# Index-key gathers of the decode tokens: begun in the last output blocks of the first feed-forward part

## The chip, the cores and the metric

The kernel runs on one core of a Trainium2 chip. The metric is the device time of one execution in microseconds (us). A core has five engines with a queue of instructions each: PE (matmuls, with its weight loads shown as PEld), DVE (elementwise on vectors), ACT (activations, also issues DMAs), POOL (elementwise, and the gathers by index) and SP (issues the weight DMAs here). Engines wait for each other by semaphores alone.

## What is computed

One layer for 256 prompt tokens and 8 decode tokens that share all weights: a half-step feed-forward part, a projection into retention, sparse attention, an indexer and gates, then the mixing and a second half-step feed-forward part.

```python
def layer_forward(x, pos, ret_state0, ret_chunk, sparse_attn, p):
    x = x + 0.5 * swiglu(rms_norm(x, ffn1_norm), ffn1_w1, ffn1_w2)
    h = rms_norm(x, mix_norm)
    rq, rk, rv, rg, aq, ak, av, iq, ik, iw, g_ret, g_att = split_cols(h @ w_in)
    ret_out, ret_state = retention(rq, rk, rv, rg, ret_state0, pos, ret_chunk, ret_norm, w_ret_out)
    ...
    att = sparse_attn(aq, ak, av, iq, iw, ik)
    merged = jax.nn.sigmoid(g_ret) * ret_out + jax.nn.sigmoid(g_att) * (att @ w_att_out)
    x = x + merged @ w_o
    x = x + 0.5 * swiglu(rms_norm(x, ffn2_norm), ffn2_w1, ffn2_w2)
```

For a decode token the sparse attention scores all 2048 earlier positions with the indexer, whose keys lie in pages of 128 positions, and the page table says which:

```python
    past_ki = pool_ki[layer, page_table].reshape(db, past, IDX_DIM)
    ki_all = jnp.concatenate([past_ki, ki], axis=1)
    idx, valid = indexer_select(qi, wi, ki_all, q_pos, n_keep)
```

## The kernel before, in words

All activations lie transposed: 128 features on the partitions, 264 tokens in the free dimension, 2048 features in 16 such blocks. `quad` (line 147) gives a tile of four blocks out of a pool of 23 equal buffers that X, the normed inputs (`hi`, `lo`), the hidden values (`hh`, `hl`), the index keys (`kt`), and the projected IQ, RK and so on share.

`mblock` (line 237) makes one output block. For every eight rows of 128 weights SP loads a piece (`wr`, L247), ACT rounds it to the high part (`wh`, L248), DVE subtracts for the low part (`wl`, L249), and PE runs three matmuls per 128 rows (L252 to L254: high by high, low by high, high by low) into one of three result buffers in PSUM (`psm`, line 137). Loads and splits carry a priority that lets them run ahead, with four buffers each.

`ffn` (line 306) goes through 44 hidden blocks in three chunks (16, 16, 12). A chunk makes its hidden blocks, two projections of 16 rows each, and then 16 output blocks m with the chunk's rows (12 in the last chunk, thus 36 matmuls a block). The function handed in, `out1` (line 346), adds the result to X[m] (L348, DVE), and in the last chunk also makes block m of the next normed input (`mixn.add`: ACT L283, DVE L284) and of its sum of squares (`mixn.square`: ACT L291, then POOL adds it into `acc`, L292).

Behind the feed-forward part comes the projection, one `mixblock` of 48 matmuls per output block: first the ik block, then `mixn.done()`, which turns `acc` into `rstd` by a matmul, two activations (L258, L259) and three operations on DVE (L262 to L264); POOL multiplies `rstd` into `cosr` and `sinr` (L383, L384). Every later block is multiplied by `rstd` as it is taken from PSUM. Eight iq blocks follow (L395 into IQ), eight rk blocks with a rotary step that ends in an addition on POOL (L876 into RK), eight rq blocks, and so on.

The index keys of the 8 decode tokens, 16 pages each, come by 64 gathers on POOL (L365, `load_kt`): a gather fetches one page for two tokens, 128 rows of 512 bytes, into one of eight `kt` tiles of eight gathers each. Their order is `kt_order`. In the source five gathers stand behind each iq block (40) and eight behind each of the first three rk blocks (24). Their addresses (`kix`) are there from the start of the kernel. The first readers are the scoring matmuls of `decode_index` (L499), which is stepped from the fourth rk block on.

The order in which each engine takes its instructions is settled before the run by the framework's planner, from the source's order, the priorities and its own estimates of durations. An instruction whose inputs are there may be moved ahead of others; a tile's first writer also needs a free buffer.

Of the kernel before, what the change touches and what calls it, by code (L numbers as in the profile page):

```python
# [19 lines left out]
P = 128  # L20
# [16 lines left out]
PG = 128  # L37
# [85 lines left out]
def layer(ctx: ExitStack, tc: tile.TileContext, xT, gains, consts, dmat, didx, pt, state, cidx, ck, cv,  # L123
          w1a, w2a, wik, win, wro, wao, wo, w1b, w2b,
          yT, o_st, o_k, o_v, o_ik, o_sts):
    nc = tc.nc
# [16 lines left out]
    def nm(s):  # L143
        cnt[0] += 1
        return f"{s}_{cnt[0]}"

    def quad(dt=F32, shape=(P, 4, T), s="q"):
        return qpool.tile(list(shape), dt, tag="q", name=nm(s))
# [4 lines left out]
    def wt(s="w", shape=(P, T), dt=F32, tag="w", bufs=8):  # L153
        return work.tile(list(shape), dt, tag=tag, name=nm(s), bufs=bufs)

    def mt(s, shape=(P, 384), dt=F32):
        return work.tile(list(shape), dt, tag="m", name=nm(s), bufs=8)

    def st(shape, dt=F32, tag="s", bufs=4):
        return small.tile(list(shape), dt, tag=tag, name=nm(tag), bufs=bufs)  # L160
# [57 lines left out]
    kix = cpool.tile([P, 4, NPG], I32, name="kix")  # L218
# [12 lines left out]
    def ahead():  # L231
        return tc.high_priority(offset=AHEAD)
# [73 lines left out]
    def ffn(norm, w1, w2, out, early=0, tick=None):  # L306
        for ci, (j0, j1) in enumerate(CHUNKS):
            n = j1 - j0
            hh, hl = Blocks(n, F32R, "hh"), Blocks(n, F32R, "hl")
            for j in range(j0, j1):  # L310
                pg = mblock(w1[2 * j], KB, norm.hi, norm.lo)
                if j < early:
                    c = wt("c")
                    nc.scalar.activation(c, pg, AF.Copy)
                    pg = c
                if j == 0:
                    rstd = norm.done()
                g = wt("g")
                nc.vector.tensor_mul(g, pg, rstd)
                s = wt("s")  # L320
                nc.scalar.activation(s, g, AF.Silu)  # L321
                s2 = wt("s2")
                nc.gpsimd.tensor_mul(s2, s, rstd)  # L323
                pu = mblock(w1[2 * j + 1], KB, norm.hi, norm.lo)
                if j < early - 1:
                    c = wt("c")
                    nc.scalar.activation(c, pu, AF.Copy)
                    pu = c
                h = wt("h")
                nc.vector.tensor_mul(h, pu, s2)  # L330
                split(h, hh[j - j0], hl[j - j0])
                if tick:
                    tick()
            for m in range(KB):
                ps = mblock(w2[m][:, j0:j1, :], n, hh, hl)
                out(m, ps, ci == len(CHUNKS) - 1)
# [6 lines left out]

    mixn = Norm("gm")

    def out1(m, ps, last):
        with ahead():
            nc.vector.scalar_tensor_tensor(X[m], ps, 0.5, X[m], op0=ALU.mult, op1=ALU.add)  # L348
        if last:
            with ahead():  # L350
                mixn.add(m, X[m])
                mixn.square(m, X[m])
            if m % 4 == 3:
                nc.scalar.dma_start(xs[:, m - 3:m + 1, :], X.t[m // 4])

    ffn(norm, w1a, w2a, out1, early=1)

    KT = [[quad(shape=(P, 1024 + h), s="kt") for h in range(2)] for _ in range(4)]
    kt_order = [(p, 8 * h + i) for h in range(2) for p in range(4) for i in range(8)]

    def load_kt(n):
        for _ in range(n):
            p, pg = kt_order.pop(0)
            o = (pg % 8) * PG
            nc.gpsimd.indirect_dma_start(out=KT[p][pg // 8][:, o:o + PG], out_offset=None, in_=cidx,  # L365
                                         in_offset=bass.IndirectOffsetOnAxis(ap=kix[:, p, pg:pg + 1], axis=0))


    def mixblock(src, m=P):
        return mblock(src, KB, mixn.hi, mixn.lo, m)  # L370
# [22 lines left out]
    for i in range(8):  # L393
        ps = mixblock(blocks["iq", i])
        nc.vector.tensor_mul(IQ[i], ps, rstd)  # L395
        load_kt(5)

    queues = {}
    slack = dict(a=60, b=100, c=130)
# [17 lines left out]
    def step(**rates):  # L417
        for n, r in rates.items():
            q = queues[n]
            q[1] += r  # L420
            while q[1] >= 1.0:
                q[1] -= 1.0
                run_one(n)
# [49 lines left out]
    def decode_index():  # L473
        for p in range(4):
            for s in range(2):
                r = slice(64 * s, 64 * s + 64)
                nc.vector.tensor_copy(KT[p][1][r, 1024:1025], ik2[r, TP + 2 * p + s:TP + 2 * p + s + 1])
        qs = st([P, NB, IH], tag="qs", bufs=1)
# [14 lines left out]
        for c0, w in spans:  # L493
            pi = aux()
            half, o = (0, c0) if c0 < 1024 else (1, c0 - 1024)
            with ahead():
                for p in range(4):
                    q2 = qs[:, 2 * p:2 * p + 2, :].rearrange("p b h -> p (b h)")
                    nc.tensor.matmul(pi[32 * p:32 * p + 32, :w], q2, KT[p][half][:, o:o + w], start=True, stop=True)  # L499
            rl = mt("drl", (P, w))  # L500
# [370 lines left out]
    def rotary(ps, out, mul):  # L871
        a, b = wt("ra"), wt("rb")
        nc.vector.scalar_tensor_tensor(a, ps, mul, cosr, op0=ALU.mult, op1=ALU.mult)
        nc.vector.scalar_tensor_tensor(b[:64], ps[64:], mul, sinr[64:], op0=ALU.mult, op1=ALU.mult)
        nc.vector.scalar_tensor_tensor(b[64:], ps[:64], mul, sinr[:64], op0=ALU.mult, op1=ALU.mult)
        nc.gpsimd.tensor_add(out, a, b)  # L876
# [146 lines left out]
    for i in range(RH):  # L1023
        ps = mixblock(blocks["rk", i])
        rotary(ps, RK[i], SCALE)
        if kt_order:
            load_kt(min(8, len(kt_order)))
        step(a=1.5, b=2 if i > 2 else 0)
    lo_pool[0] = (1, 2)
    for i in range(RH):  # L1030
# [79 lines left out]
    for i in range(16):  # L1110
# [3 lines left out]
        s = wt("s")  # L1114
# [124 lines left out]
```

## Time and profile before

| | us |
|---|---|
| median of 3 runs | 2736.94 |
| lowest and highest | 2730.61, 2738.26 |
| profiled execution | 2738.78 |
| its span, first to last instruction | 2736.7 |
| PE busy in it | 2634.1 |
| POOL busy in it | 658.3 |

The span is that of the profiled execution alone. The share of busy time is a mean over the whole span; where an engine makes others late is seen in a stretch, from the count of its instructions, the waits ahead of them, and the granted clock of PE (1.00 is 2.4 GHz, 0.50 is 1.2 GHz).

### The profile page before, as it was taken

To read this page: it belongs to the slowest core of one execution; us is meant where nothing else is said; L and a number is where in the kernel's file an instruction comes from. 1 tells how busy PE (TensorE), PEld (TensorE's weight loads), DVE (VectorE), ACT (ScalarE), POOL (GpSimd) and SP (SyncE) were. 2 spreads that over 40 slices of the span, in tenths; PEclk is the share of its full clock that TensorE was granted. 3 is DMA by queue.
4 is the path that set the end of the run, shared out by engine and by line. 5 is a ranking of instruction groups with operands and counts; after the bars stand their busy time and mean duration, and the time that the engine had idled before them with its cause. 6 is when DMAs were issued, how large, how long until landed. Compare 5 with 4: busy or idle time off the path is not lost. (4 is left out here: it accounts for less than half of the span.)

```text
span 2736.7 us, 51339 instructions
## 1 busy us (share of the span) xinstructions
PE 2634.1 (96%) x21207; PEld 2594.1 (95%) x21207; DVE 1561.2 (57%) x2288; ACT 1173.8 (43%) x1557; POOL 658.3 (24%) x459
## 2 busy tenths in 40 slices
PE   7999999999997899999997999999999999999999
PEld 7999999999996699899887989999999999999999
DVE  6555555545553488644699744566655555555554
ACT  5443344334452333353535754444544334433443
POOL 3110011001135443326377243231111101110110
PEclk9999999999997899999998999999999999999999
DMA  6556555655564344456686656666576656765655
GB/s 214 182 181 182 181 183 180 184 178 184 172 222 132 106 157 160 140 174 229 216 274 217 198 190 217 203 203 220 177 235 228 216 183 226 234 215 183 214 170 171
DMA packets 173963, 529.08 MB, mean 193 GB/s; under 512 B 22704, under 2 KB 43760, under 8 KB 173728
## 3 DMA queue, kind: packets, MB, share of 16 engines
q1 hardware_dynamic: 140320, 466.28, 52.7%
q10 hardware_dynamic: 27504, 43.92, 4.9%
q0 software_dynamic: 5904, 15.59, 1.7%
q8 instruction: 166, 2.72, 0.4%
q14 instruction: 69, 0.57, 0.1%
HBM read 504.12 MB, written 21.60 MB: 192 GB/s over the span
## 5 line engine op out<-in xcount | busy, mean ns | idle before, releaser
L248 ACT ACTIVATE wh<-wr 128x1024 fp32r<-128x1024 f32 x866 | 902.4, 1043 | 1314.0 <-PE ps L253 839.1
L249 DVE TENSOR_TENSOR wl<-wr,wh 128x1024 fp32r<-128x1024 f32 (+2 forms) x798 | 993.4, 1246 | 672.2 <-ACT wh L248 651.1
L254 PE MATMUL ps<-hi,wl 128*128 128x264 f32 x4624 | 1329.3, 288 | 29.2 <-DVE wl L249 16.5
L252 PE MATMUL ps<-hi,wh 128*128 128x264 f32 x4624 | 1328.5, 287 | 29.1 <-issue 11.9
L253 PE MATMUL ps<-lo,wh 128*128 128x264 f32 x4624 | 1332.8, 288 | 11.2 <-issue 9.4
L254 PEld LDWEIGHTS ps<-hi,wl 128*128 128x128 f32 x4624 | 877.7, 190 | 39.8 <-DVE wl L249 19.8
L252 PEld LDWEIGHTS ps<-hi,wh 128*128 128x128 f32 x4624 | 879.6, 190 | 33.6 <-issue 19.2
L253 PEld LDWEIGHTS ps<-lo,wh 128*128 128x128 f32 x4624 | 878.4, 190 | 21.3 <-issue 17.1
L254 PE MATMUL ps<-hh,wl 128*128 128x264 f32 x1408 | 398.8, 283 | 0.0
L253 PE MATMUL ps<-hl,wh 128*128 128x264 f32 x1408 | 398.5, 283 | 0.0
L252 PE MATMUL ps<-hh,wh 128*128 128x264 f32 x1408 | 398.3, 283 | 0.0
L323 POOL TENSOR_TENSOR s<-s,rstd 128x264 f32<-128x264 f32 x88 | 116.9, 1329 | 1009.8 <-ACT s L321 1009.8
L253 PEld LDWEIGHTS ps<-hl,wh 128*128 128x128 f32 x1408 | 264.6, 188 | 0.0
L252 PEld LDWEIGHTS ps<-hh,wh 128*128 128x128 f32 x1408 | 264.5, 188 | 0.0
L254 PEld LDWEIGHTS ps<-hh,wl 128*128 128x128 f32 x1408 | 264.3, 188 | 0.0
L249 POOL TENSOR_TENSOR wl<-wr,wh 128x1024 fp32r<-128x1024 f32 x68 | 166.9, 2459 | 299.7 <-ACT wh L248 251.1
L805 POOL TENSOR_TENSOR pr<-qb,kb 128x1024 f32<-128x1024 f32 x32 | 86.0, 2705 | 60.0 <-DMA qb<-rows 51.6
L938 POOL TENSOR_TENSOR kv<-ku,rvs 128x512 f32<-128x512 f32 x32 | 33.6, 1051 | 219.6 <-DMA ku<-rows 206.4
L940 DVE SCALAR_TENSOR_TENSOR su<-su,kv 128x256 f32<-128x256 f32 x64 | 24.4, 422 | 98.2 <-POOL kv L938 98.2
L292 POOL TENSOR_TENSOR acc<-acc,sq 128x264 f32<-128x264 f32 x45 | 40.8, 906 | 154.0 <-ACT sq L291 153.1
L330 DVE TENSOR_TENSOR h<-ps,s 128x264 f32<-128x264 f32 x88 | 38.0, 432 | 64.5 <-PE ps L254 61.1
L253 PE MATMUL ps<-alo,wh 128*128 128x264 f32 x256 | 72.7, 284 | 0.0
(317 smaller groups left out, 2356.7 us busy)
## 6 DMA issues: line engine op xcount, KB each, us to landing
wr<-win SPq DMA_DIRECT2D x224, 512.0 KB
wr<-w1a SPq DMA_DIRECT2D x176, 512.0 KB
wr<-w1b SPq DMA_DIRECT2D x176, 512.0 KB
wr<-w2a SPq DMA_DIRECT2D x80, 512.0 KB
wr<-w2b SPq DMA_DIRECT2D x80, 512.0 KB
wr<-wro SPq DMA_DIRECT2D x32, 512.0 KB
wr<-wao SPq DMA_DIRECT2D x32, 512.0 KB
wr<-wo SPq DMA_DIRECT2D x32, 512.0 KB
```

What stands on the lines that cost most here:

```text
L248: nc.scalar.activation(wh[:, :n, :m], wr[:, :n, :m], AF.Copy)
L249: eng.tensor_sub(wl[:, :n, :m], wr[:, :n, :m], wh[:, :n, :m])
L252: nc.tensor.matmul(ps[:m, :T], wh[:, k, :m], hi[g], start=g == 0, stop=False)
L253: nc.tensor.matmul(ps[:m, :T], wh[:, k, :m], lo[g], start=False, stop=False)
L254: nc.tensor.matmul(ps[:m, :T], wl[:, k, :m], hi[g], start=False, stop=g == nk - 1)
L292: nc.gpsimd.tensor_add(self.acc, self.acc, sq)
L323: nc.gpsimd.tensor_mul(s2, s, rstd)
L330: nc.vector.tensor_mul(h, pu, s2)
L805: nc.gpsimd.tensor_mul(pr, qb, k.to_broadcast([P, 2, 4, P]))
L938: nc.gpsimd.tensor_mul(kv, k[:, :, None, :].to_broadcast([P, 2, 2, P]), v.to_broadcast([P, 2, 2, P]))
L940: nc.vector.scalar_tensor_tensor(s[:, i], s[:, i], g1[h + i], kv[:, i], op0=ALU.mult, op1=ALU.add)
```

## The change

`load_kt`, its list and its eight tiles move ahead of `out1`; a tile is now taken from the pool when its first gather is issued, not all eight at once. `out1` issues two gathers per output block of the last chunk (32 in 16 blocks), an iq block three and not five (24 in eight blocks), and an rk block up to three and not eight (8 in three blocks). Order, addresses and targets of the gathers stay.

```diff
     mixn = Norm("gm")
 
+    KT = [[None, None] for _ in range(4)]
+    kt_order = [(p, 8 * h + i) for h in range(2) for p in range(4) for i in range(8)]
+
+    def load_kt(n):
+        for _ in range(min(n, len(kt_order))):
+            p, pg = kt_order.pop(0)
+            o = (pg % 8) * PG
+            if KT[p][pg // 8] is None:
+                KT[p][pg // 8] = quad(shape=(P, 1024 + pg // 8), s="kt")
+            nc.gpsimd.indirect_dma_start(out=KT[p][pg // 8][:, o:o + PG], out_offset=None, in_=cidx,
+                                         in_offset=bass.IndirectOffsetOnAxis(ap=kix[:, p, pg:pg + 1], axis=0))
+
     def out1(m, ps, last):
...
             if m % 4 == 3:
                 nc.scalar.dma_start(xs[:, m - 3:m + 1, :], X.t[m // 4])
+            load_kt(2)
 
     ffn(norm, w1a, w2a, out1, early=1)
-
-    KT = [[quad(shape=(P, 1024 + h), s="kt") for h in range(2)] for _ in range(4)]
-    kt_order = [(p, 8 * h + i) for h in range(2) for p in range(4) for i in range(8)]
-
-    def load_kt(n):
...
         nc.vector.tensor_mul(IQ[i], ps, rstd)
-        load_kt(5)
+        load_kt(3)
...
         rotary(ps, RK[i], SCALE)
-        if kt_order:
-            load_kt(min(8, len(kt_order)))
+        load_kt(3)
         step(a=1.5, b=2 if i > 2 else 0)
```

## Rows read from the trace of the kernel before

**Rows 1.** The page: busy us, PE in 40 slices with its clock, the chain.

```profile
PE 2634.1 (96%) x21207; PEld 2594.1 (95%) x21207; DVE 1561.2 (57%) x2288; ACT 1173.8 (43%) x1557; POOL 658.3 (24%) x459
...
PE   7999999999997899999997999999999999999999
...
PEclk9999999999997899999998999999999999999999
...
PE 40%; DMA 1%; issue 0%; POOL 0%; ACT 0%; DVE 0%
```

**Rows 2.** Stretches: length, busy us (xinstructions) of PE, PEld, DVE, ACT, POOL; clock, DMA, GB/s.

```profile
700.00:760.00 60.00, 60.00 (x498) 60.00 (x497) 34.07 (x49) 30.12 (x47) 7.65 (x9) 1.00 0.58 180
802.00:820.00 18.00, 18.00 (x150) 18.00 (x150) 9.03 (x10) 6.37 (x6) 14.49 (x13) 1.00 0.66 218
820.00:837.10 17.10, 13.55 (x80) 10.97 (x80) 6.68 (x12) 3.18 (x3) 13.45 (x12) 0.97 0.52 170
837.10:857.50 20.40, 7.58 (x21) 5.53 (x21) 1.23 (x1) 1.06 (x1) 15.50 (x17) 0.50 0.25 78
857.50:861.30 3.80, 1.37 (x4) 0.61 (x3) 0.00 (x0) 0.00 (x0) 0.00 (x0) 0.50 0.05 17
861.30:867.00 5.70, 5.70 (x27) 5.70 (x28) 2.88 (x3) 2.12 (x2) 0.00 (x0) 0.53 0.34 112
...
898.00:913.50 15.50, 6.65 (x29) 4.86 (x27) 3.18 (x6) 1.06 (x1) 11.96 (x14) 0.70 0.27 85
913.50:917.30 3.80, 1.31 (x5) 1.15 (x5) 0.00 (x0) 0.00 (x0) 1.60 (x2) 0.50 0.11 35
917.30:922.00 4.70, 4.70 (x25) 4.70 (x25) 3.45 (x5) 2.12 (x2) 0.97 (x1) 0.58 0.24 73
1144.00:1154.00 10.00, 10.00 (x73) 9.55 (x72) 2.48 (x6) 3.59 (x6) 7.58 (x8) 1.00 0.26 80
...
1515.60:1525.00 9.40, 9.40 (x78) 9.35 (x77) 9.23 (x16) 8.86 (x13) 7.50 (x6) 1.00 0.81 258
```

**Rows 3.** PE's timeline in the hole: start, length, instruction, idle before and its releaser.

```profile
844.33 0.58 PE L254 MATMUL ps<-hi,wl 128*128 128x264 f32 x1 [1.03 <-issue]
...
845.75 0.38 PE L253 MATMUL ps<-lo,wh 128*128 128x264 f32 x1 [0.62 <-issue]
```

**Rows 4.** POOL's timeline from cosr to the second rk addition and the last gather.

```profile
801.02 0.77 POOL L383 TENSOR_TENSOR cosr<-C,rstd 128x264 f32<-128x264 f32 x1 [8.89 <-DVE rstd L264]
...
802.65 1.85 POOL L365 DMA_INDIRECT kt<-cidx,kix  x1
...
856.53 0.95 POOL L365 DMA_INDIRECT kt<-cidx,kix  x1 [0.30 <-issue]
...
880.76 1.79 POOL L876 TENSOR_TENSOR rk<-ra,rb 128x264 f32<-128x264 f32 x1 [23.28 <-DVE rb L875]
882.70 0.96 POOL L365 DMA_INDIRECT kt<-cidx,kix  x1
...
905.00 0.75 POOL L876 TENSOR_TENSOR rk<-ra,rb 128x264 f32<-128x264 f32 x1
...
913.40 0.94 POOL L365 DMA_INDIRECT kt<-cidx,kix  x1 [0.30 <-issue]
```

**Rows 5.** Gathers: ns min/median/max of all 64; the first 40, busy us, mean ns, idle.

```profile
L365 POOL DMA_INDIRECT kt<-cidx,kix x64: 940/945/1949, 802.7 to 913.4; - x64
...
L365 POOL DMA_INDIRECT kt<-cidx,kix x40 | 42.9, 1073 | 12.0 <-issue 11.6 <-PE ps L254 0.3
```

**Rows 6.** Timelines of POOL (first and last square added), DVE (rstd), PE (third iq block).

```profile
730.26 0.76 POOL L292 TENSOR_TENSOR acc<-acc,sq 128x264 f32<-128x264 f32 x1 [14.72 <-ACT sq L291]
...
791.37 0.76 POOL L292 TENSOR_TENSOR acc<-acc,sq 128x264 f32<-128x264 f32 x1 [3.96 <-ACT sq L291]
...
800.50 0.43 DVE L264 SCALAR_TENSOR_TENSOR rstd<-t,rstd 128x264 f32<-128x264 f32 x1
...
806.93 0.28 PE L252 MATMUL ps<-hi,wh 128*128 128x264 f32 x1
```

More of the change, by code (lines that the diff above doesn't have):

```diff
@@ L354, in out1 @@
                 nc.scalar.dma_start(xs[:, m - 3:m + 1, :], X.t[m // 4])
+            load_kt(2)
     ffn(norm, w1a, w2a, out1, early=1)
-    KT = [[quad(shape=(P, 1024 + h), s="kt") for h in range(2)] for _ in range(4)]
-    kt_order = [(p, 8 * h + i) for h in range(2) for p in range(4) for i in range(8)]
-    def load_kt(n):
[L362 to L366, printed above, removed]
     def mixblock(src, m=P):
```

## Prediction

> **What bounds the kernel now.** I read the page first. PE is busy 96% of the span, and 40% of the chain that ended last are three matmul lines in equal parts [rows 1]. So a change of POOL's work pays only where POOL makes PE late. Then the page's slices, which show where PE dips, and for the dip behind 820 us the busy-time table by stretch: the granted clock falls to 0.50 there, and the matmuls can be counted [rows 2]. Undisturbed PE starts 498 in 60 us, 8.30 a us [rows 2]. From 802 to 820 it still starts 150 in 18 us, which is full rate. Then 80 in 17.1 us, 21 in 20.4 us and 4 in 3.8 us, after which 27 in 5.7 us at half clock [rows 2]. At full rate these four stretches hold 142, 169, 32 and 47. The missing 62, 148, 28 and 20 make 258, or 31.1 us. A second hole follows: 29 in 15.5 us, 5 in 3.8 and 25 in 4.7, so 100, 26 and 14 are missing, 140 or 16.9 us [rows 2]. Together 48.0 us.
>
> What does PE wait for there? The timeline puts its idle time down to "issue", waiting for nothing that the profile shows, with about 1.4 us between starts that are 0.12 us apart elsewhere [rows 3]. It isn't bandwidth: the DMA share is 0.25 in the worst stretch, against 0.58 where PE runs freely [rows 2]. What coincides is POOL. Its timeline has 40 index-key gathers in one unbroken run, from 802.65 to 857.5, and 24 more from 882.70 to 914.3 with one addition among them [rows 4]. PE falters some 17 us into each run and recovers 3 to 4 us after its last gather (PE is back at 861.3 and 917.3). Six value gathers in a row from 1515.6 cost nothing: 78 matmuls in 9.4 us is full rate [rows 2]. In the 16 gathers from 1144 the first 10 us have 73 matmuls for 83, at most 1.2 us lost for eight [rows 2]. I read this as a store that fills while gathers follow each other and empties when they stop: the first dozen are free, and each later one costs about 1.1 us (148 matmuls, 17.9 us, over 16 gathers from 837.1 to 857.5).
>
> **The change, part by part.** No gather is added or removed; all 64 stay on POOL, and so do their transfers. The length of the runs changes, and what stands behind them in POOL's queue.
>
> The engine order is fixed before the run, and it isn't the order of the source. After the rk addition at 880.76 the source has eight gathers and then the next addition; POOL ran 17 gathers first, and the next addition at 905.00 [rows 4]. So gathers move forward past other work. Yet POOL idled 23.28 us ahead of that first addition, and 8.89 us ahead of cosr, with gathers still to come [rows 4]. I take it that a gather can move forward only as far as its KT tile has got one of the 23 shared buffers, and that these are given out in the source's order, each when its first writer is due: the run of 40 starts just after the first IQ tile is due, that of 24 just after the first RK tile. With that rule I place the new runs:
>
> Out blocks. Gathers 1, 9, 17 and 25 open a tile, in the blocks m = 0, 4, 8, 12, behind that block's new hi and lo tiles. So I expect four runs of eight, not two per block. The additions of the squares stand 4.365 us apart (15 from 730.26 to 791.37) [rows 6], so a run may start each 17.5 us. A gather costs (42.9 + 12.0)/40 = 1.37 us with the gap behind it [rows 5], a run 11.0 us, which leaves 6.5 us to empty the store. Cost to PE: nothing by the first dozen gathers of the run of 40 and by the six value gathers, at most 1.2 us a run by the 16; I take 0, nearest to the row of the same gather. What they hold up: POOL's additions into acc stand behind a run. The last run starts near 778.3 and ends near 789.3, then the additions 13 to 15 follow at 0.76 us each; the last starts near 791.6, against 791.37 now. The chain from it to rstd (at 800.9) thus moves by less than 1 us. The cover: with three result buffers PE can finish the ik block and two iq blocks before it needs rstd, until 806.93 [rows 6], 6.0 us. Beyond that each us costs one.
>
> Here a rule stands against the change. The gathers move beside a busy DVE (34.07 of 60 us [rows 2]); beside DVE's subtractions they took up to 1.95 us, with DVE idle 0.94 [rows 5]. At 1.95 plus the 0.30 gap throughout, a run takes 18.0 us, the last addition starts near 798, and rstd comes at 808, 1 us past the cover; by these rows the sum rises by 1 us at most. The Trainium skill ("SBUF — State Buffer", section "SBUF: two separate sides") says that GpSimd can't write its descriptors while a DVE instruction holds the port pair that they share, and gives 3.1 us for a transfer that takes 0.62 alone. By that figure, an estimate of the page, a gather would take 4.7 us, the four runs 150 us, and the sum would end near 2780. The trace agrees with the direction, at twice the time and not five times.
>
> iq blocks. 24 gathers remain here, three per block in the source. Gather 33 opens a tile behind IQ's first, 41 in block 2, 49 in block 5 behind IQ's second tile. No other POOL work lies between sinr and the first rk addition, so in POOL's queue the 24 stand together and run back to back from some 802.6. Their cost: the first 24 of the 40 end at 837.1 with 62 matmuls missing; emptying costs 28 (857.5 to 861.3), the half clock behind it 14 to 20. That is 104 to 110, or 12.5 to 13.3 us. The other run of 24 cost 16.9. I take 13, as the place and the gathers are the same.
>
> rk blocks. Eight gathers remain behind the first rk addition: one run, cost 0 by the same rows. The first rk addition isn't held up: the 24 end near 836, and its input comes from a block that ends after 850.
>
> The sum. The profiled execution took 2738.8 us (span 2736.7). Off go 48.0, on come 0 + 13 + 0: 2703.8. The median of the runs is 1.8 below the profiled one: **2702**, with 0 to 6 us more for five runs of eight, 0 to 4 more for the run of 24, and 6 less as the lowest run of before lies under its median: 2696 to 2712. Is the time kept further on? PE is at full rate where nothing disturbs it, and DVE is idle in the holes (1.23 us busy of 20.4 [rows 2]), so no work that the holes now hide becomes late.
>
> **The rivals.**
> (a) Runs as the source spaces them: two per 4.4 us, three per 5.8 us, never more than three together. Then the run of 24 costs nothing: 2702 - 13 = 2689. For it: the pace that the source asks for is below what stalled. Against: POOL ran 17 where the source has eight [rows 4].
> (b) The 32 of the out blocks stay in one run, because the later hi and lo tiles come first in line. From 24 to 40 gathers the loss grows by 31.1 - 13 = 18 us, 1.13 each; 32 cost 22 us, and rstd, late behind them, finds PE late too: 2724.
> (c) The cost goes with the number of gathers, not with the run: 48.0/64 = 0.75 us each wherever they are: 2737, no change. Against: the value gathers and the first dozen of each run.
> (d) Slower: the store doesn't empty between runs. Its emptying was seen only with POOL silent and PE nearly still (4 matmuls in 3.8 us); in the out blocks PE runs at full rate. If 6.5 us don't empty a run of eight, from the second run on every gather pays 1.1: 52 x 1.1 = 57 us in place of 48, and half clock behind each of up to five runs, 2.4 us (20 matmuls) each: 2746 to 2758, say 2750. It decides where PE, at full rate, takes more than 6.5 us to shed the backlog.
> (e) Starved gathers: if a gather beside a busy DVE takes over 2.3 us, the last addition comes late and PE stops for rstd past 806.93. At twice the worst row (4.5 us with the gap), 32 gathers from 726 end at 870, rstd at 882, 75 us past the cover: some 2775. The Trainium skill's page named above would have it so. No row of the trace is longer than 1.95.
>
> **How the numbers follow.** The forecast has 0.50: the rule for the buffers explains where both runs start, but is read off those two alone. (a) 0.15, (b) 0.11, (c) 0.10, (d) 0.12, (e) 0.02. A measurement here tells apart some 0.3%, 8.2 us. Faster: forecast, (a) and (b), 0.76. Same: (c), 0.10. Slower: (d) and (e), 0.14. The range 2684 (5 below (a), for the same scatter) to 2737 holds the forecast, (a), (b) and half of (c), 0.81; the forecast's own stays 2696 to 2712.
>
> **What would show it.** In the profile after: POOL's timeline with runs of 8, 8, 8, 8 between 726 and 790, one of 24 from about 802, one of eight behind the first rk addition. The table by stretch at 8.3 matmuls a us through the out blocks, a hole of some 13 us that begins near 820, and none near 850 to 890 (the rk blocks, now earlier). rstd within 1 us of 800.9. Wrong if matmuls are missing in the out blocks (d), if PE waits for rstd near 807 (b, e), if the iq run leaves no hole (a), or if 48 us of holes stand elsewhere (c).

## The result and the profile after

The change made the kernel faster by about what was forecast: 2693.5 us (median of four runs, 2687.8 to 2697.3) against 2737.6 us (four runs, 2730.6 to 2742.8), ratio 0.984 with an interval of 0.981 to 0.987. The profiled execution took 2693.0 us, its span 2691.0. The forecast was 2702, its own range 2696 to 2712; the time lies 2.5 us under that range and inside the wide one. The experiments show that the stall which the prediction rests on is there in some sessions only, and that this pair was measured in one of them. Times are medians of a kernel's runs; one run of eight of the changed kernel in session 3, at a granted clock of 0.85, took 2825.9 us and is compared with nothing here.

First the page's busy line of PE after the change, then the busy-time table by stretch (columns as in [rows 2]: length, then busy us and instructions of PE, PEld, DVE, ACT, POOL, then clock, DMA share, GB/s).

```profile
PE 2613.1 (97%) x21207; PEld 2580.8 (96%) x21207; DVE 1569.1 (58%) x2288; ACT 1171.5 (44%) x1557; POOL 667.3 (25%) x459
```

```profile
700.00:760.00 60.00, 59.53 (x490) 59.17 (x490) 34.95 (x48) 29.35 (x45) 26.84 (x27) 1.00 0.63 190
730.00:789.00 59.00, 59.00 (x489) 59.00 (x489) 40.45 (x56) 33.79 (x55) 38.65 (x38) 1.00 0.77 241
802.00:820.00 18.00, 18.00 (x150) 18.00 (x149) 11.76 (x18) 7.53 (x8) 14.88 (x12) 1.00 0.67 214
820.00:840.00 20.00, 19.86 (x156) 18.93 (x155) 8.88 (x13) 5.53 (x6) 15.40 (x14) 1.00 0.64 203
840.00:853.00 13.00, 12.62 (x104) 12.64 (x105) 9.08 (x16) 5.24 (x6) 1.31 (x1) 1.00 0.63 208
```

Read the counts at 8.30 matmuls a us [rows 2]. In the out blocks (730 to 789) PE starts 489 in 59 us: full rate, with 24 gathers beside it. Just before, beside the first run of eight, 8 are missing (490 where 498 stood from 700 to 760), 1.0 us. Beside the iq run 156 stand where 166 fit, and 104 where 108 fit: 14 missing, **1.7 us**. In the kernel before 258 were missing there [rows 2], 31.1 us. The clock stays at 1.00; it was 0.50.

POOL's timeline after the change, where its runs begin and end:

```profile
715.28 1.04 POOL L355 DMA_INDIRECT kt<-cidx,kix  x1 [0.17 <-issue]
...
791.92 0.75 POOL L292 TENSOR_TENSOR acc<-acc,sq 128x264 f32<-128x264 f32 x1 [2.78 <-ACT sq L291]
801.50 0.77 POOL L385 TENSOR_TENSOR cosr<-C,rstd 128x264 f32<-128x264 f32 x1 [8.83 <-DVE rstd L264]
...
803.12 1.79 POOL L355 DMA_INDIRECT kt<-cidx,kix  x1
...
818.00 1.77 POOL L355 DMA_INDIRECT kt<-cidx,kix  x1 [0.30 <-issue]
...
838.49 0.95 POOL L355 DMA_INDIRECT kt<-cidx,kix  x1 [0.30 <-issue]
851.69 1.73 POOL L878 TENSOR_TENSOR rk<-ra,rb 128x264 f32<-128x264 f32 x1 [12.25 <-DVE rb L877]
853.56 0.96 POOL L355 DMA_INDIRECT kt<-cidx,kix  x1
```

They are runs of eight from 715.28, 740.45, 758.22 and 775.76 (the last three with one addition inside), one of 24 from 803.12 to 839.43, and one of eight behind the first rk addition. cosr stands at 801.50, where it stood at 801.02 [rows 4].

### The profile page after: what moved, and what is told of

It reads as the page before. It is cut to its first block, busy times and chain, and to the rows that moved or that the text cites. A ratio compares the mean times of both kernels' runs of the same rounds, so it can differ in the third digit from the quotient of the medians.

```text
span 2691.0 us, 51338 instructions
## 1 busy us (share of the span) xinstructions
PE 2613.1 (97%) x21207; PEld 2580.8 (96%) x21207; DVE 1569.1 (58%) x2288; ACT 1171.5 (44%) x1557; POOL 667.3 (25%) x459
## 4 chain that ended last, share of the span: by engine, by line
PE 81%; DVE 6%; DMA 4%; issue 3%; ACT 3%; POOL 2%; another core or an unknown queue 0%; ACTq 0%; DVEq 0%; POOLq 0%; SPq 0%
PE ps L253 26%; PE ps L252 26%; PE ps L254 26%; DVE wl L249 2%; DVE junk L539 1%; ACT wh L248 1%; DMA sb<-state 1%; POOL sb L912 1%; DMA wr<-win 1%; DMA vb<-cv,rowi 0%; POOL wl L249 0%; POOL pr L807 0%; DMA qb<-rows 0%; DVE psc L759 0%; DMA ku<-rows 0%
## 5 line engine op out<-in xcount | busy, mean ns | idle before, releaser
L355 POOL DMA_INDIRECT kt<-cidx,kix x64 | 73.4, 1147 | 18.1 <-issue 17.1
L252 PE MATMUL ps<-ahi,wh 128*128 128x264 f32 x256 | 72.7, 284 | 0.0
```

The costliest lines, as they stand in the source:

```text
L252: nc.tensor.matmul(ps[:m, :T], wh[:, k, :m], hi[g], start=g == 0, stop=False)
```

## The experiments

Kernels that were run together share a session: one chip, and runs of the kernel before beside them. There were six sessions, the pair above being the first. The kernel before did not take the same time in all of them:

| session | kernel before, us | kernels run beside it: median us, ratio with its interval |
|---|---|---|
| 1 | 2737.6 | changed kernel 2693.5, 0.984 (0.981 to 0.987) |
| 2 | 2698.3 | e1_dep 2750.2, 1.019 (1.017 to 1.020); e3_iq24 2696.8, 1.000 (0.999 to 1.001); e2_iq32 2684.2, 0.994 (0.993 to 0.996); e6_half 2730.8, 1.011 (1.009 to 1.013) |
| 3 | 2697.9 | before2 2699.5, 1.001 (1.000 to 1.002); after2 2683.3, 0.995 (0.993 to 0.996); e4_out32 2706.4, 1.004 (1.002 to 1.005); e5_out64 2707.2, 1.004 (1.002 to 1.005) |
| 4 | 2742.2 | e9_rkdve 2761.8, 1.008 (1.005 to 1.011); e10_after_rkdve 2713.7, 0.989 (0.984 to 0.993) |
| 5 | 2699.2 | e11_paced32 2698.0, 0.999 (0.998 to 1.000) |
| 6 | 2743.2 | e12_paced4 2696.5, 0.982 (0.979 to 0.985) |

So there are two kinds of session, near 2698 and near 2740 for the same kernel, and each experiment has to be read with its kind.

**The same two kernels again (before2, after2).** No edit; session 3.

> The kernel before once more, with a profile. Among the experiments so far it took 2692.9 to 2705.1 us in 13 runs on one chip, where it had taken 2730.6 to 2742.8 us in four runs beside the changed kernel. The mechanism of the prediction (a run of 40 gathers makes PE late wherever it stands) expects the two holes of 48 us in every execution: 2730 to 2743, and POOL's run of 40 from 802 with PE falling behind from 820. If the stall needs something beyond the run of gathers that differs from chip to chip, or from load to load of the program, then it can come out near 2698, with the same run of 40 on POOL and PE near full rate beside it.

> The changed kernel once more, on the same chip as the kernel before. By the mechanism of the prediction 2688 to 2697 again, 44 us below the kernel before. If the stall depends on the chip, then on a chip where the kernel before has no holes the change can gain only what little is left: the ratio to the kernel before is 0.995 to 1.0 there, and 0.984 on a chip with the holes.

The stretches of before2, then those of after2:

```profile
802.00:850.00 48.00, 48.00 (x397) 48.00 (x396) 28.28 (x39) 18.03 (x17) 38.09 (x34) 1.00 0.72 228
850.00:880.00 30.00, 30.00 (x227) 27.46 (x226) 21.85 (x40) 11.39 (x15) 24.04 (x22) 1.00 0.58 191
880.00:900.00 20.00, 9.54 (x69) 7.86 (x67) 4.94 (x9) 3.89 (x6) 14.48 (x17) 0.81 0.30 96
```

```profile
802.00:850.00 48.00, 48.00 (x397) 48.00 (x396) 28.68 (x43) 17.77 (x17) 30.65 (x26) 1.00 0.67 221
850.00:880.00 30.00, 30.00 (x240) 28.35 (x239) 20.40 (x37) 12.28 (x16) 16.09 (x13) 1.00 0.51 169
880.00:900.00 20.00, 20.00 (x147) 13.31 (x146) 10.18 (x19) 7.55 (x13) 2.70 (x2) 1.00 0.33 110
```

Here the kernel before has the same run of 40 gathers (POOL is busy 38.09 of 48 us), and PE starts 397 matmuls in 48 us beside it, 8.27 a us, as after2 does: **the run alone costs nothing**. What the change gains here, 14.6 us, lies later. From 880 to 900 PE starts 69 matmuls here and 147 in after2; followed matmul by matmul through the lines 252 to 254, before2 is 1.7 us behind after2 at 880 and 15.5 us at 900. ACT's timeline of before2, then POOL's, then DVE's and PE's show why:

```profile
879.85 1.06 ACT L248 ACTIVATE wh<-wr 128x1024 fp32r<-128x1024 f32 x1 [1.87 <-PE ps L253]
896.36 0.26 ACT L1040 ACTIVATE rks<-rk 128x32 f32<-128x32 f32 x1 [15.46 <-POOL rk L876]
896.50 1.04 ACT L248 ACTIVATE wh<-wr 128x1024 fp32r<-128x1024 f32 x1
```

```profile
860.89 1.83 POOL L876 TENSOR_TENSOR rk<-ra,rb 128x264 f32<-128x264 f32 x1
862.88 0.96 POOL L365 DMA_INDIRECT kt<-cidx,kix  x1 [0.16 <-issue]
...
885.51 0.76 POOL L876 TENSOR_TENSOR rk<-ra,rb 128x264 f32<-128x264 f32 x1
...
894.88 2.83 POOL L876 TENSOR_TENSOR rk<-ra,rb 128x264 f32<-128x264 f32 x4
```

```profile
897.57 1.24 DVE L249 TENSOR_TENSOR wl<-wr,wh 128x1024 fp32r<-128x1024 f32 x1 [9.95 <-ACT wh L248]
898.73 0.15 DVE L489 TENSOR_TENSOR w<-aux,C 128x8 f32<-128x8 f32 x1
...
898.94 1.64 PE L446 MATMUL aux<-ik,iq 64*128 64x128 f32 x4 [10.46 <-DVE w L489]
```

Read it backwards. PE waits 10.46 us for a small DVE operation (`w`, line 489), which stands behind a subtraction in DVE's queue. The subtraction waits 9.95 us for a converted weight; ACT converts none from 880.91 to 896.50, because ahead of the next conversion in its queue stands a small copy (rks, line 1040) that wants the results of four rk additions; those stand on POOL behind 17 and then seven gathers. In after2 the same copy waits 2.29 us. This is a plain queue, read from the waits: late POOL, then ACT, DVE and PE.

**One run of 32 in the iq blocks (e2_iq32).** The changed kernel with

```
-        load_kt(3)
+        load_kt(5)
```

in the iq loop. Session 2.

> The changed kernel with five gathers for each iq block in place of three: the 24 of the iq blocks and the eight of the rk blocks become one run of 32. By the length of the run at 1.1 us for each gather beyond the first dozen: 22 us in the iq blocks, against 1.4 measured for 24, so 2693 + 20 = 2713. By a store that sheds at a fixed rate: PE's loss starts only when the backlog has reached the loads that PE reads, near the 20th gather in the changed kernel, so eight more cost at most 8 x 1.1 plus the emptying of 4 us: 2695 to 2706. By a price for each gather: no change, 2693.

2684.2 us, as after2 (2683.3) against the same kernel before. From 802 to 850 PE starts 397 in 48 us beside 32 gathers on end. Both expectations of a loss fell; the session was of the other kind.

**No gathers in the out blocks (e3_iq24).** The changed kernel without `load_kt(2)` in out1, and `load_kt(20)` in place of `load_kt(3)` in the rk loop. Session 2.

> The changed kernel without gathers in the out blocks: 24 stand in the iq blocks, as in the changed kernel, and the other 40 behind the first rk additions, 20 for each of two blocks. It asks why the run of 24 cost 1.4 us in the changed kernel, where the first 24 gathers of the run before cost 7.5 us by their end and 13 with the emptying. If it matters that they were the first gathers of this kind (no run ahead of them), the first 24 cost 7 to 13 us here as before, with PE falling behind from about 815. If it is the length of the run alone, or small differences in spacing (1.43 us before, 1.51 after), the 24 cost 1 to 3 us. The 40 behind them, at 1.1 us for each beyond the first dozen, cost about 31 us as in the kernel before; by a price of 0.75 us for each gather all 64 cost 48. Times: 2693 + 31 - 1 = 2723 with a cheap run of 24, 2735 with a dear one, 2737 by the price for each gather.

2696.8 us. The 24 in the iq blocks cost nothing (397 in 48 us), so that question stays open there. With 40 behind the first rk additions the time is that of the kernel before, but by another path than in before2: ACT's copy waits 1.4 us only, and PE waits 4.5 us for late keys (line 500), with conversions that wait for PE in turn. So late gathers in the rk blocks cost as much as gathers ahead of additions; the times of e2 and e3 alone don't tell the two apart.

**A long run in one out block (e4_out32), all 64 in the out blocks (e5_out64).** `if m == 12: load_kt(32)`, and `load_kt(4)`, in place of `load_kt(2)` in out1. Session 3.

> The changed kernel with its 32 gathers of the out blocks put into one block (m = 12): on POOL runs of 6, 13 and 13 with one addition into acc between them, ahead of the last additions. It is the rival of one long run. Where a long run makes PE late (1.13 us for each gather beyond the first dozen, and rstd late behind them): 2715 to 2724. Where it doesn't, only rstd is late: the 32 gathers at 1.4 us from some 774 end near 820, the last addition comes near 822 and rstd at 831 in place of 800.9, and PE, covered until 806.9, stands for 24 us: 2717 on either kind of chip, with PE's idle time put down to rstd or a result buffer, not to issue.

> The changed kernel with all 64 gathers in the out blocks (four per block): on POOL 16 together, then runs of 8 to 13 with one addition into acc between them, and the last nine additions behind the last gather. 64 gathers at 1.4 us from 715 and seven additions end near 810, nine additions at 0.76 us by 817, rstd at 826: 19 us past the cover of 806.9, so PE stands there for some 19 us, less the 0 to 8 us that the emptied iq and rk blocks give back: 2695 to 2712. If gathers that follow each other with only single additions between them make PE late in the out blocks (1.1 us each from the second dozen on), add up to 57 us: 2750.

2706.4 and 2707.2. In both PE stands for rstd; its longest wait from 795 to 870, e4 first:

```profile
PE auxm L296 <- POOL acc L292: 15.9, 1, 15.9
```

```profile
PE auxm L296 <- POOL acc L292: 12.6, 1, 12.6
```

So the additions into acc are the danger in the out blocks, as the prediction has it under its second and fifth rival. I expected 2717 for e4 because I added the 24 us to the time of session 1; from after2's 2683.3 they make 2707. In e5 PE starts 662 matmuls from 720 to 800, full rate, beside runs of 16, 13, 3, 13 and 13 gathers with single additions between them; the session was one without the stall, so this says nothing of the stall.

**Half of the rows (e6_half).** The kernel before, where each gather fetches 64 of its 128 rows and DVE fills the other half of each KT tile with 0 (the second token of each pair is left out). Session 2.

```
+    for p in range(4):
+        for h in range(2):
+            nc.vector.memset(KT[p][h][64:], 0.0)
...
-            nc.gpsimd.indirect_dma_start(out=KT[p][pg // 8][:, o:o + PG], ...
+            nc.gpsimd.indirect_dma_start(out=KT[p][pg // 8][:64, o:o + PG], ...
```

> The kernel before with each gather fetching 64 rows in place of 128 (the first token of each pair; the keys of the second one are set to 0 by DVE at the start, so half of the index keys are left out). The 64 gathers keep their places and their POOL time if that is a fixed cost. If the store holds rows or their descriptors, half as many fill it half as fast, it never overflows, and the two holes of 48 us shrink to under 10: 2690 to 2700. If the cost is in the instruction on POOL (a number of gathers, however many rows they have), the holes stay: 2730 to 2737.

2730.8 us, and no answer to the question: the fills became the tiles' first writers, the gathers moved forward to 774.67 with the additions into acc behind them, and PE waited 30.8 us for acc. What it does show is the prediction's rule for the order: give a tile its buffer earlier, and its gathers are hoisted to there.

**Pacing all 64 gathers (e1_dep).** In the kernel before, a POOL multiplication ahead of each gather, reading the slice that was filled two gathers earlier. Session 2.

```
+            dst = KT[p][pg // 8][:, o:o + PG]
+            kt_done.append(dst)
+            if len(kt_done) > 2:
+                nc.gpsimd.tensor_mul(dst, kt_done[-3], ident)
```

> The kernel before, with all 64 gathers where they were, but from the third on a POOL multiplication (128x128, reading the slice that the gather two before filled) stands ahead of each gather and writes the slice that the gather then overwrites. So a gather can't be issued before the one two ahead of it has landed: nothing changes but the spacing. Store that sheds at a fixed rate (spacing decides): at a spacing of 1.6 us or more PE loses next to nothing in either run, the two holes of 48 us go, and the time is 2690 to 2700. Price by length of run (1.1 us for each gather beyond the first dozen, whatever the spacing): the runs are as long as before, 2737. Price by gather (0.75 us each wherever it stands): 2737. If the spacing becomes 2 us or more, the 64 gathers take until about 935, and the first rk addition may stand behind some of them: up to 15 us on top of the first theory's time.

2750.2 us. The session hadn't the stall, so spacing could gain nothing, and it delayed the rk additions (the first seven come between 896.85 and 957). The longest waits from 870 to 960 are the queue of before2 made worse:

```profile
ACT rks L1046 <- POOL rk L882: 38.9, 1, 38.9
...
PE ps L252 <- ACT wh L248: 18.5, 1, 18.5
```

**Nothing behind the gathers (e9_rkdve, e10_after_rkdve).** The kernel before, and the changed kernel, with the addition in rotary on DVE. Session 4, one of 2742.

```
-        nc.gpsimd.tensor_add(out, a, b)
+        nc.vector.tensor_add(out, a, b)
```

> The kernel before with the addition that ends each rotary block (line 876) done by DVE in place of POOL. No gather moves, but nothing stands behind gathers on POOL any more, so all 64 follow each other from 802 to some 895. Theory of the order (where the kernel before takes 2698 us, its loss near 885 to 900 is DVE waiting for rk additions that stand behind 24 gathers on POOL, and PE behind DVE): the loss goes, 2698 - 14 = 2684, as in the changed kernel, with a run of 64 gathers and PE at full rate beside it. Theory of the long run (the prediction's: a run itself makes PE late, 1.13 us for each gather beyond the first dozen): a run of 64 costs more than the runs of 40 and 24 together, so no gain, and where the kernel before takes 2737, some 2737 - 48 + 31 + 24 x 1.13 = 2747.

> The changed kernel with the same edit: eight gathers stand ahead of the second rk addition in the changed kernel, and PE loses some 6 us from 850 to 910. If those 6 us are still the order on POOL, the time falls by up to 6 us, 2683 to 2677. If they are the small matmuls of the index work, nothing changes, or DVE's six to seven additions of 0.43 us take up to 3 us of its time: 2683 to 2686. The theory of the long run expects one run of 32 in the iq blocks: 2683 to 2706.

2761.8 and 2713.7. Now all 64 gathers of e9 follow each other, and 32 of e10, with no POOL work behind them that anyone waits for. The stretches of e9, then of e10:

```profile
820.00:840.00 20.00, 14.70 (x86) 12.39 (x86) 6.61 (x12) 3.18 (x3) 15.56 (x15) 0.90 0.47 152
840.00:887.30 47.30, 9.62 (x26) 7.29 (x26) 1.23 (x1) 1.06 (x1) 36.03 (x38) 0.50 0.21 64
887.30:895.00 7.70, 2.19 (x6) 1.47 (x6) 0.31 (x1) 1.15 (x2) 0.00 (x0) 0.50 0.03 9
```

```profile
805.00:830.00 25.00, 25.00 (x208) 25.00 (x207) 15.81 (x25) 9.31 (x9) 20.27 (x17) 1.00 0.69 231
830.00:851.00 21.00, 12.77 (x64) 9.85 (x63) 2.88 (x3) 2.12 (x2) 16.03 (x17) 0.70 0.39 127
851.00:856.00 5.00, 3.02 (x13) 2.76 (x13) 0.76 (x1) 1.29 (x2) 0.00 (x0) 0.50 0.04 13
```

In such a session the run itself does make PE late, and no queue of POOL's work is needed for it. e9 misses 80, 367 and 58 matmuls, 60.8 us; e10 misses 110 and 28, 16.7 us. With the changed kernel and the kernel before of session 1: a run of 24 costs 1.7 us, 32 cost 16.7, 40 cost 31.1, 64 cost 60.8 (four kernels in two sessions). Once PE has nearly stopped each further gather costs its own 1.24 us (38 gathers in 47.30 us, in which PE starts 26). What e9 was to test as well, whether the 14 us go when nothing stands behind the gathers, it couldn't show in a session with the stall; the queue of before2 stays a reading of its waits, with which e1_dep agrees.

ACT's timeline shows what goes wrong. First the kernel before in session 1, then before2:

```profile
807.01 1.06 ACT L248 ACTIVATE wh<-wr 128x1024 fp32r<-128x1024 f32 x1 [1.85 <-PE ps L253]
809.93 1.06 ACT L248 ACTIVATE wh<-wr 128x1024 fp32r<-128x1024 f32 x1 [1.87 <-PE ps L253]
814.35 1.06 ACT L248 ACTIVATE wh<-wr 128x1024 fp32r<-128x1024 f32 x1 [3.35 <-PE ps L254]
...
827.71 1.06 ACT L248 ACTIVATE wh<-wr 128x1024 fp32r<-128x1024 f32 x1 [3.41 <-PE ps L254]
831.49 1.06 ACT L248 ACTIVATE wh<-wr 128x1024 fp32r<-128x1024 f32 x1 [2.72 <-PE ps L254]
844.35 1.06 ACT L248 ACTIVATE wh<-wr 128x1024 fp32r<-128x1024 f32 x1 [11.80 <-remote]
```

```profile
806.91 1.06 ACT L248 ACTIVATE wh<-wr 128x1024 fp32r<-128x1024 f32 x1 [1.85 <-PE ps L253]
809.84 1.06 ACT L248 ACTIVATE wh<-wr 128x1024 fp32r<-128x1024 f32 x1 [1.87 <-PE ps L253]
...
827.36 1.06 ACT L248 ACTIVATE wh<-wr 128x1024 fp32r<-128x1024 f32 x1 [1.87 <-PE ps L253]
830.27 1.06 ACT L248 ACTIVATE wh<-wr 128x1024 fp32r<-128x1024 f32 x1 [1.85 <-PE ps L253]
```

Each conversion waits until 24 matmuls have freed a tile, 2.92 us at full rate. In before2 it keeps that step through the whole run. In session 1 the step becomes 4.4 us from the conversion at 814.35 on, although PE goes on at full rate until 820 [rows 2]. From 807.01 to 831.49 ACT has been told of six tiles, 144 matmuls, while PE started 173 (before2: eight tiles and 194, from 806.91 to 830.27):

```profile
807.01:831.49 24.48, 23.22 (x173) 21.46 (x172) 9.48 (x13) 6.36 (x6) 19.30 (x18) 1.00 0.59 196
```

So what PE has done is heard of ever later while gathers follow each other, some 29 matmuls late by 831.49, and then PE itself starts only about one matmul for each gather (21 beside 16 gathers from 837.1 to 857.5 [rows 2]).

The trace also has the time of every addition to PE's semaphore, by which PE reports a tile as used; no view prints them. Where nothing disturbs, the addition comes 0.30 us after its matmul has started. In session 1 that of the matmul at 812.53 comes at 814.33, that of 815.46 at 818.77, that of 822.21 at 827.69 and that of 830.42 at 844.32, 13.9 us after its start; each time ACT's conversion starts 0.02 us after the addition. The last one, at 844.35, which its line puts down to "remote", waited for PE's report too, and not for a late weight piece: the queue of the weight loads moved nothing from 837.13 to 847.64. Nor does a late load of code show: the queue with the 16 KB loads of code has one at 824.65 and the next at 868.53, and PE was back at 861.3 without it. That fits the store of the prediction, with PE's reports in it. Which part of the chip holds them, and why PE itself then nearly stops, the trace doesn't say.

The second hole of session 1 has the same mark. The lines of ACT:

```profile
903.14 1.06 ACT L248 ACTIVATE wh<-wr 128x1024 fp32r<-128x1024 f32 x1 [5.26 <-remote]
917.40 2.25 ACT L248 ACTIVATE wh<-wr 128x1024 fp32r<-128x1024 f32 x2 [13.21 <-remote]
...
929.58 0.24 ACT L1040 ACTIVATE rks<-rk 128x32 f32<-128x32 f32 x1
```

PE's reports for the matmuls at 896.30 and 899.21 come at 903.11 and 917.38, and the two conversions start 0.02 us behind them. The copy `rks`, on which the queue of before2 turned, waits for nothing here.

One more thing sets the two kinds of session apart. In all five traces of sessions 1, 4 and 6, additions to semaphores are missing from the record where gathers run (PE's semaphore lacks 9 to 30 of some 1966); in the nine others PE's lacks none. The kernel before in session 1 has 252 of 252 of its four engines' additions from 710 to 800, ahead of its gathers, and 130 of 159 from 800 to 930; the changed kernel has 202 of 250 from 710 to 800, where its gathers now run. The paced kernel below lacks them too, without being late. So the changed kernel's run of session 1 was one with the stall. Every run here has a span and a granted clock on record, thus was recorded while it ran; whether the stall is there without the recording is an open rival.

**The run of 32, paced (e11_paced32, e12_paced4).** e10 with the multiplication of e1_dep in the run of 32: in e11 from the 35th gather on, each waiting for the one two ahead, in e12 from the 37th on, each waiting for the one four ahead (its edit is shown):

```
+            if len(kt_done) > 36:
+                nc.gpsimd.tensor_mul(dst, kt_done[-5], ident)
```

> The changed kernel with DVE doing the rk additions, so that 32 gathers stand together in the iq blocks, and with a POOL multiplication (128x128, reading the slice that the gather two before filled, writing the slice that is filled next) ahead of each of them from the third on. No gather can be issued before the one two ahead has landed, which in the paced kernel of the first experiment made a mean spacing of near 2 us in place of 1.42. The same run of 32 without pacing cost 18 us on a chip where the kernel before takes 2742 us, and 2713.7 in all. If spacing decides: on such a chip the loss beside the run goes, 2690 to 2697, and ACT's conversions of weights stay 2.92 us apart. If the number of gathers in the run decides: 2710 to 2715, as without pacing. On a chip where the kernel before takes 2698 us both expect 2681 to 2687: there pacing can only be seen to cost nothing.

> As the paced kernel before it, but each gather of the run of 32 waits for the one four ahead of it in place of two, since waiting for two made a mean spacing of 3.2 us and the last keys late (PE stood 7.4 us for them). Four ahead should give 1.6 to 1.8 us, and the last gather at 853 to 860, before the keys are wanted. Where the kernel before takes 2698 us: 2682 to 2688, PE at full rate beside the run, as the changed kernel. Where the kernel before takes 2742 us: if spacing decides, 2690 to 2698 and ACT's conversions stay 2.92 us apart; if the number of gathers decides, 2710 to 2715, as the same run without pacing.

e11 (session 5, no stall): 2698.0. Its spacing became 3.1 us, and PE waited 7.4 us for late keys, so pacing that hard costs some 14 us. e12 (session 6, kernel before 2743.2): **2696.5**, where the unpaced e10 took 2713.7 beside 2742.2. Its 32 gathers start from 803.72 to 876.1, 2.33 us apart against 1.44 in e10 (805.33 to 849.96). The part of the run beside the iq blocks in e12, the stretch of the whole run, and two of ACT's conversions in it:

```profile
803.00:850.00 47.00, 47.00 (x389) 47.00 (x388) 28.74 (x41) 18.02 (x17) 38.90 (x38) 1.00 0.64 209
803.00:877.00 74.00, 74.00 (x590) 71.46 (x589) 50.85 (x78) 28.31 (x31) 60.61 (x61) 1.00 0.60 195
```

```profile
834.35 1.06 ACT L248 ACTIVATE wh<-wr 128x1024 fp32r<-128x1024 f32 x1 [1.86 <-PE ps L253]
837.26 1.06 ACT L248 ACTIVATE wh<-wr 128x1024 fp32r<-128x1024 f32 x1 [1.84 <-PE ps L253]
```

The step is 2.92 us in the timeline read (805 to 846), PE starts 389 matmuls in 47 us, full rate, and it is busy all 74 us. Followed matmul by matmul, e10 falls 19.9 us behind after2 from 830 to 860, e12 1.4 us. With 32 gathers between the same two pieces of other work, pacing took the stall away, so their number alone isn't the cause. The pacing changed three things at once: the spacing, the gathers under way (four at most), and a POOL multiplication between gathers; which of them counts isn't shown. The two were also timed in different sessions of the same kind. No kernel tried beats the changed one in both kinds: e2 equals it without the stall, and e12 lies about where it lies with it.

## Why the prediction was right, and where it wasn't

**What bounds the kernel before.** Both holes were read rightly for session 1: PE's reports come late while gathers follow each other, some way into each run, and PE recovers when the run ends. What the prediction didn't see is that the run isn't enough. In session 3 the same run of 40 costs nothing (before2), and by the kernel's time it can't have cost much in sessions 2 and 5. Nothing in the one trace could have told, but the claim "a long run makes PE late" was made for the kernel, where it holds for some executions of it. That the pair fell into a session with the stall is luck: without it the change gains 14.6 us, and most of what the prediction takes off isn't there to gain.

**The second hole** (16.9 us) was put down to the store as well, and in session 1 that holds: ACT waited for PE's late reports there. In sessions without the stall a hole stands in nearly the same place that is a queue: rk additions behind gathers, ACT's copy behind them, the weight conversions behind that. The row that points there was on the table, the second addition at 905.00 behind 17 gathers [rows 4]; the prediction didn't ask who waits for that addition. In session 1 ACT's copy came without a wait for it, and DVE waited for PE's report (904.56), not for POOL.

**The sum.** Off 48.0 was right within session 1. Followed matmul by matmul, the kernel before is 0.5 us ahead of the changed one at 800, 30.2 us behind at 860 and 48.0 us behind from 880 to 960, so both holes went; by the end of the span it is 45.7 us behind (medians: 44.1). Where the 2 to 3 us between were lost again the runs don't show.

**The run of 24** is the term that was mis-sized: 13 us forecast, 1.7 measured. These 11.3 us, less the 2 to 3 us lost again later, are the 8.5 us by which the forecast was too high. I took the loss of the first 24 of the 40 (62 matmuls) and added emptying and half clock, 42 to 48 more. But the rows were of another pace. In the kernel before the tenth gather starts at 815.88, 1.47 us apart from 802.65 on; after the change at 818.00, 1.65 apart from 803.12 on, beside a DVE that is busy 11.76 us of 18 and not 9.03. ACT's step grows to 4.4 us only with the conversion at 829.43, not at 814.35 (one step of 3.3 us, at 816.63, is made up by the next), so the run of 24 ends (839.43) just when PE begins to falter, and emptying and half clock never come. e10 has the same pace and the same late start, and its eight gathers more cost 15 us; e9 has the pace and the early start of the kernel before. Those four agree, but the two slower ones also have 32 gathers in the out blocks behind them, so the pace isn't singled out. A price taken from the first part of a longer run wants the same pace and the same past.

**The places of the runs.** The rule for the buffers held: 24 in one run and eight behind the first rk addition, and in the out blocks runs that open with a tile. Each of these four began earlier than forecast, the first by 11 us, ahead of m = 0's own hi and lo tiles, and three let one addition in between. It cost 1.0 us, beside the first run; PE is at full rate beside the other three, and the last addition starts at 791.92, where I expected some 791.6.

**acc, rstd and the cover.** Less than 1 us was forecast; cosr moved by 0.5. The longest gather is 1.94 us, as in the kernel before (1.95 [rows 5]); the 4.7 us that an estimate from the Trainium skill ("SBUF — State Buffer", section "SBUF: two separate sides") gave is seen in no run here, so its 2780 fell. That estimate took the ratio of two times that the Trainium skill gives there. The same section of the Trainium skill says that the wait lasts until the DVE instruction ends, which gives no such ratio, and the trace agrees with that: of the 28 gathers after the change that took over 1.1 us, 27 end 0.80 to 0.84 us after a DVE operation that they overlapped.

**The rivals.** (a), no loss in the run of 24, came nearer in its result (2689, 4.5 us off) than the forecast (8.5) without its reason: the runs weren't spaced. (b) would have met rstd late, as e4 shows. (c) fell: 64 gathers cost 0 or 48 or 61 us by session and pace. (d) fell: beside the four runs of eight in the out blocks PE lost 1.0 us in all, at full clock, in session 1. (e) fell with the longest gather.

## What to carry over

Before blaming a resource for a hole, ask of each instruction that stands late in a queue who waits for it: where there is no stall, nearly all of the gain is a few POOL additions that no longer stand behind gathers, while in session 1 ACT's copy of their result waited for none of them. A run of gathers on POOL is best broken by other work or spread over stages with slack; where it can't be, pacing to 2.3 us was harmless where 1.4 us cost 17 us in a run of 32, and too wide a spacing (3.1 us) made the data late. A stall that one trace shows should be looked for in a second session before its whole price goes into a sum.

## What was unexpected

The same kernel has two times, 2698 and 2740 us, and no session mixes them (29 runs from 2693.1 to 2703.6 in one, 11 from 2728.5 to 2753.6 in another). Whether the chip decides it or something set up with the session stays open: one chip number stands in the results with either time. That PE's progress is reported up to 29 matmuls late, with PE down to about one matmul for each gather, shows only where ACT's waits are set against PE's count, or the semaphore's times against the matmuls; PE's own idle time names no cause, and "remote" hid it.
